# Four of the eleven gate-and-up pairs of each FFN by one level of Strassen's scheme

## The chip, the cores and the metric

The kernel runs on one core of a Trainium2 chip. Its time is the device time of one execution in microseconds (us); shorter is better. The engines that matter here are PE (TensorE, the matmuls), DVE (VectorE) and ACT (ScalarE), which work on tensors in on-chip memory, and the queues that issue transfers: SP (SyncE) for loads and POOL (GpSimd) for stores. Each engine goes through its own list of instructions in order, and waits where one needs what another engine or a transfer has not finished.

## The reference

Two decoder layers over 512 tokens of width 1024, all in float32. Layer 0 mixes tokens by causal pooling, layer 1 by differential attention; each layer ends in a feed-forward network (FFN) of 2816 hidden features. The change is in the FFN alone:

```python
def _swiglu(x, w_gate, w_up, w_down):
    return (jax.nn.silu(x @ w_gate) * (x @ w_up)) @ w_down

for i in range(DEPTH):
    mixed = pool(x) if i % 2 == 0 else diff_attention(x)
    x = _layernorm(ALPHA * x + mixed, ...)
    x = _layernorm(ALPHA * x + _swiglu(x, w_gate[i], w_up[i], w_down[i]), ...)
```

## The kernel before

**Precision.** Every float32 operand is split into a high part (a cast on ACT, L89) and a low part (a subtraction on DVE, L90); a product is three matmuls: high by high, high by low, low by high (`mm3`, L107 to L110).

**Layout.** Activations stand transposed: `xt` holds the layer's input as [feature of a block of 128, token half, high or low, block, 256 tokens]. The weights lie in `wall` as pieces of 128x1024. `fetch` loads a piece from `wall` on SP into one of RAWS = 4 `raw` tiles, `ready` splits it into one of WBUFS = 6 pairs of tiles `wh`, `wl`. A raw tile is free again once its piece is split, a pair of split tiles once the product that reads it is done.

**The FFN** (`ffn`, from L436) has two stages. In the first, the 2816 hidden features are 22 blocks `f` of 128, taken in pairs k and k + 11 (11 pairs). A block has one gate piece and one up piece; `product` multiplies each with all 512 tokens in 24 matmuls of 128x128 by 128x512 into one bank. `gated` applies silu on ACT (L459) and the multiply on DVE (L460) and leaves the block in `hid`. The first blocks ("early", 3 in layer 0, 2 in layer 1) are done in token halves of 256 columns, since the second half of the tokens comes late. The remaining blocks are the loop at L587; after a product it splits a further piece, five ahead.

In the second stage the down projection already runs by one level of Strassen's scheme: the seven products P1, Q5, P6, Q3, P7, P2, Q4, each over six groups of rows (`items`). What it needs is made during the first stage, in the shadow of PE's matmuls:

- `sum_weights(k)`: sums of quarters of the down weights for row block k. Four loads `b` on SP (L482), four DVE adds of 128x512 (L484), four stores to `tsum` in device memory on POOL's queue (L486). The four `b` tiles are single, so a load of one set waits for the store of the same tile in the set before. It runs for one k in every other feature, and besides at the first and the last of the loop (L597).
- `sum_hidden(k)`: sums of quarters of `hid` for pair k. A copy of one quarter to `a11` on ACT (L497), five DVE operations of 128x256 (L498 to L504), the cast `v` on ACT (L505), and, deferred to `settle` in the next feature, the low part on DVE (L508) and a store to `ssum` (L509).
- `affine`: scale and shift of the residual `res` by the layer norm's parameters, two DVE operations of 128x1024 (L189, L190) in each of the four features after the first of the loop.

In the down stage `prepare` fetches and splits the items five ahead, and `left` splits their left sides out of `hid` into `xt`, or loads them from `ssum`; for P1 `a11` is used as it stands.

The order on each engine is the order in which the code issues: nothing is reordered afterwards.

Of the kernel before, what the change touches and what calls it, by code (L numbers as in the profile page):

```python
# [45 lines left out]
DOWN = ("P1", "Q5", "P6", "Q3", "P7", "P2", "Q4")  # L46
PAIRS = [(0, 2), (2, 2), (4, 2), (6, 2), (8, 2), (10, 1)]
# [3 lines left out]
def trunk(ctx, tc, x, wall, pscale, lam_p, subln, table, lng, lnb, band, first, onehot, out):  # L51
# [381 lines left out]

    ROWS = [slice(k, k + n) for k, n in PAIRS]

    def ffn(layer, late):  # L436
        n = 2 * layer + 1
        final = n == 2 * DEPTH - 1
        c0 = base[0]
        with tc.tile_pool(name=f"ffn{layer}", bufs=1) as fp:  # L440


            hid = fp.tile([P, FB, S], F32, name=f"hid{layer}")
            a11 = fp.tile([P, 2, HALF, 256], F32R, name=f"a11_{layer}")

            def product(acc, c, lo, hi):
                h, l = weights(c)
                for k in range(KB):
                    mm3(
                        wide(acc, lo, hi),  # L450
                        (h[:, k * P : (k + 1) * P], l[:, k * P : (k + 1) * P]),
                        x_at(k, lo, hi),
                        k == 0,
                        k == KB - 1,
                    )

            def gated(f, pg, pu):
                sg = keep.tile([P, S], F32, tag="y", name=f"sg{layer}_{f}", bufs=2)
                nc.scalar.activation(sg, pg, AF.Silu)  # L459
                nc.vector.tensor_tensor(hid[:, f, :], sg, pu, op=ALU.mult)  # L460

            c1 = c0 + 2 * FB
# [11 lines left out]
            def sum_weights(k):  # L474

                i, j = k // 2, k % 2
                c = slice(j * 512, (j + 1) * 512)
                b11, b12, b21, b22 = t = [
                    fp.tile([P, 512], F32, tag=f"b{b}", name=f"b{b}_{layer}_{k}") for b in range(4)
                ]  # L480
                for b in range(4):
                    nc.sync.dma_start(out=t[b], in_=block(i, b)[:, c])  # L482
                for z, x, y in ((b11, b11, b12), (b12, b12, b22), (b22, b11, b22), (b21, b22, b21)):
                    nc.vector.tensor_tensor(z, x, y, op=ALU.add)  # L484
                for m, z in enumerate((b11, b22, b12, b21)):
                    nc.gpsimd.dma_start(out=tsum[m, i, :, c], in_=z)  # L486

            late_low = []
            summed_rows = [0]

            def sum_hidden(k):
                first, second = hid[:, k, :256], hid[:, k, 256:]
                a12, a22 = hid[:, k + HALF, :256], hid[:, k + HALF, 256:]
                u = fp.tile([P, 2, 256], F32, tag="u", name=f"u{layer}_{k}", bufs=1)
                v = fp.tile([P, 2, 2, 256], F32R, tag="v", name=f"v{layer}_{k}", bufs=1)
                tt = nc.vector.tensor_tensor
                nc.scalar.copy(a11[:, 0, k, :], first)  # L497
                tt(second, second, a22, op=ALU.subtract)  # L498
                tt(a11[:, 1, k, :], first, a11[:, 0, k, :].bitcast(F32), op=ALU.subtract)
                tt(first, second, first, op=ALU.subtract)  # L500
                nc.vector.scalar_tensor_tensor(
                    u[:, 0, :], first, -1.0, a22, op0=ALU.mult, op1=ALU.subtract
                )
                tt(u[:, 1, :], a12, first, op=ALU.add)  # L504
                nc.scalar.copy(v[:, :, 0, :], u)  # L505
# [11 lines left out]
            early = 3 if layer == 0 else 2  # L517
            accs = [(bank(f"g{layer}_{f}"), bank(f"u{layer}_{f}")) for f in range(early)]
            for lo in (0, 256):
                for f in range(early):  # L520
                    for i in range(2):
                        product(accs[f][i], c0 + 2 * f + i, lo, lo + 256)
                        if not lo and (f, i) in late:
                            late[f, i]()
                        if not lo:
                            ready(c0 + 2 * early)
                    if lo:
                        ready(c0 + 2 * f + 6)
                        gated(order[f], *accs[f])
            sum_hidden(0)  # L530
            if layer:
                load_gb(n - 1)
            items = [(p, i) for p in DOWN for i in range(len(PAIRS))]
            made, drops, prepared = {}, {}, [0, 0]
            fetched_items = [0]

# [19 lines left out]
            def left(j):  # L556
# [3 lines left out]
                if p == "P1":  # L560
                    made[j] += (a11[:, 0, r, :], a11[:, 1, r, :])
                    return
# [540 lines left out]
```

## Time and profile before

| what | before |
|---|---|
| time, median of 3 runs | 981.78 us (980.24 to 983.37) |
| the profiled execution's own time | 983.17 us |
| its span, first to last instruction | 981.1 us |
| mean granted clock of PE | 0.995 |
| PE busy | 963.2 us in 4974 matmuls |
| DVE busy | 643.4 us in 1007 instructions |
| ACT busy | 420.5 us in 708 instructions |
| loads of raw pieces (SP) | 128 of 512 KB, median 4.2 us from issue to landing |
| loads of `b` (SP) | 88 of 256 KB, median 5.6 us |

Layer 0's first stage runs from 40 to 284 us on PE. In a line of instructions "L90 DVE ... wl<-raw,wh" is line 90 of the kernel, the engine, and what is written and read; "x118 | 141.7, 1220 | 33.3" is 118 instances, 141.7 us busy in all, 1220 ns each, and 33.3 us in which the engine was idle just before them, with what ended that. In a timeline the first two columns are start and duration in us, and square brackets hold the idle time before.

### The profile page before, as it was taken

To read this page: it belongs to the slowest core of one execution; us is meant where nothing else is said; L and a number is where in the kernel's file an instruction comes from. 1 tells how busy PE (TensorE), PEld (TensorE's weight loads), DVE (VectorE), ACT (ScalarE), POOL (GpSimd) and SP (SyncE) were. 2 spreads that over 40 slices of the span, in tenths; PEclk is the share of its full clock that TensorE was granted. 3 is DMA by queue.
4 is the path that set the end of the run, shared out by engine and by line. 5 is a ranking of instruction groups with operands and counts; after the bars stand their busy time and mean duration, and the time that the engine had idled before them with its cause. 6 is when DMAs were issued, how large, how long until landed. Compare 5 with 4: busy or idle time off the path is not lost.

```text
span 981.1 us, 13416 instructions
## 1 busy us (share of the span) xinstructions
PE 963.2 (98%) x4974; PEld 820.6 (84%) x4974; DVE 643.4 (66%) x1007; ACT 420.5 (43%) x708; POOL 123.7 (13%) x195
## 2 busy tenths in 40 slices
PE   8999999999999999999999999999999999999995
PEld 8898888888888888988888888988888888888884
DVE  6845874455567577688777676756655555477687
ACT  5753222223326357656556554732223322244460
POOL 4201111111120211000000000011111111111102
PEclk9999999999999999999999999999999999999997
DMA  8247768655776984323222122276665566878942
GB/s 223 66 158 247 250 228 289 229 193 193 266 257 236 329 295 151 114 82 94 73 87 86 55 86 86 90 270 211 225 256 193 209 229 228 288 246 297 341 145 86
DMA packets 70079, 188.59 MB, mean 192 GB/s; under 512 B 15956, under 2 KB 16084, under 8 KB 70014
## 3 DMA queue, kind: packets, MB, share of 16 engines
q1 hardware_dynamic: 56588, 141.57, 42.1%
q0 software_dynamic: 13408, 46.15, 13.9%
q8 instruction: 39, 0.64, 0.3%
q14 instruction: 26, 0.21, 0.1%
q10 hardware_dynamic: 18, 0.02, 0.0%
HBM read 150.99 MB, written 36.72 MB: 191 GB/s over the span
## 4 chain that ended last, share of the span: by engine, by line
PE 94%; DVE 3%; ACT 1%; POOL 1%; issue 0%; POOLq 0%; DVEq 0%
PE P L629 13%; PE g L109 8%; PE u L108 8%; PE u L109 8%; PE g L108 8%; PE u L110 8%; PE g L110 8%; PE Q L629 6%; PE s L814 2%; PE v L108 2%; PE v L110 2%; PE v L109 2%; PE wo L108 2%; PE wo L109 2%; PE wo L110 2%; PE q L109 1%
## 5 line engine op out<-in xcount | busy, mean ns | idle before, releaser
L90 DVE TENSOR_TENSOR wl<-raw,wh 128x1024 fp32r<-128x1024 f32 x118 | 141.7, 1220 | 33.3 <-ACT wh L89 33.3
L89 ACT CAST wh<-raw 128x1024 fp32r<-128x1024 f32 x120 | 123.5, 1050 | 65.9 <-PE u L109 63.9
L109 PE MATMUL g<-xt,wh 128*128 128x512 f32 (+1 forms) x392 | 144.1, 368 | 0.5 <-DVE xt L90 0.5
L108 PE MATMUL g<-xt,wh 128*128 128x512 f32 (+1 forms) x392 | 144.3, 368 | 0.0
L108 PE MATMUL u<-xt,wh 128*128 128x512 f32 (+1 forms) x392 | 144.1, 368 | 0.0
L110 PE MATMUL u<-xt,wl 128*128 128x512 f32 (+1 forms) x392 | 144.0, 367 | 0.0
L109 PE MATMUL u<-xt,wh 128*128 128x512 f32 (+1 forms) x392 | 144.0, 367 | 0.0
L110 PE MATMUL g<-xt,wl 128*128 128x512 f32 (+1 forms) x392 | 144.0, 367 | 0.0
L460 DVE TENSOR_TENSOR hid<-sg,u 128x512 f32<-128x512 f32 x44 | 30.3, 688 | 154.9 <-PE u L110 154.5
L90 DVE TENSOR_TENSOR dl<-r,dh 128x1024 fp32r<-128x1024 f32 x84 | 94.3, 1132 | 38.8 <-ACT dh L89 38.7
L89 ACT CAST dh<-r 128x1024 fp32r<-128x1024 f32 x84 | 81.5, 979 | 69.6 <-PE P L629 31.7
L629 PE MATMUL P<-dh,xt 128*128 128x512 f32 x352 | 109.4, 390 | 0.0
L109 PEld LDWEIGHTS g<-xt,wh 128*128 128x128 f32 x392 | 73.9, 189 | 12.7 <-DVE xt L90 0.7
L110 PEld LDWEIGHTS u<-xt,wl 128*128 128x128 f32 x392 | 73.9, 189 | 12.3
L108 PEld LDWEIGHTS u<-xt,wh 128*128 128x128 f32 x392 | 73.9, 189 | 12.1
L110 PEld LDWEIGHTS g<-xt,wl 128*128 128x128 f32 x392 | 73.9, 188 | 12.2
L108 PEld LDWEIGHTS g<-xt,wh 128*128 128x128 f32 x392 | 73.9, 188 | 12.2
L109 PEld LDWEIGHTS u<-xt,wh 128*128 128x128 f32 x392 | 73.9, 188 | 12.0
L505 ACT CAST v<-u 128x512 fp32r<-128x512 f32 x22 | 13.7, 621 | 159.4 <-issue 142.5
L629 PEld LDWEIGHTS P<-dh,xt 128*128 128x128 f32 x352 | 66.1, 188 | 13.6
L484 DVE TENSOR_TENSOR b<-b,b 128x512 f32<-128x512 f32 x88 | 60.8, 691 | 18.4 <-DMA b<-in_wall 16.2
L459 ACT ACTIVATE sg<-g 128x512 f32<-128x512 f32 x44 | 26.3, 599 | 103.5 <-PE g L110 102.0
(189 smaller groups left out, 1792.5 us busy)
## 6 DMA issues: line engine op xcount, KB each, us to landing
raw<-in_wall SPq DMA_DIRECT2D x128, 512.0 KB, 4.2
b<-in_wall SPq DMA_DIRECT2D x88, 256.0 KB, 5.6
tsum<-b POOLq DMA_DIRECT2D x88, 256.0 KB, 4.7
r<-tsum SPq DMA_DIRECT2D x40, 512.0 KB, 4.7
r<-in_wall SPq DMA_DIRECT2D x30, 512.0 KB, 5.0
ssum<-v POOLq DMA_DIRECT2D x22, 512.0 KB, 4.0
xt<-ssum POOLq DMA_DIRECT2D x20, 512.0 KB, 6.0
res<-in_x SPq DMA_DIRECT2D x8, 256.0 KB, 6.4
```

The lines of the kernel that those rows point to most:

```text
L89: nc.scalar.copy(dst_h, src)
L90: (low or nc.vector).tensor_tensor(dst_l, src, dst_h.bitcast(F32), op=ALU.subtract)
L108: nc.tensor.matmul(acc, ah, bh, start=start, stop=False)
L109: nc.tensor.matmul(acc, ah, bl, start=False, stop=False)
L110: nc.tensor.matmul(acc, al, bh, start=False, stop=stop)
L459: nc.scalar.activation(sg, pg, AF.Silu)
L460: nc.vector.tensor_tensor(hid[:, f, :], sg, pu, op=ALU.mult)
L484: nc.vector.tensor_tensor(z, x, y, op=ALU.add)
L505: nc.scalar.copy(v[:, :, 0, :], u)
L629: nc.tensor.matmul(accs[s], x[:, k, r], y[:, c], start=first and k == 0 and e == 0, stop=last and k == m - 1 and e == 2, skip_group_check= ...
L814: nc.tensor.matmul(accs[c][:, :wide], a[r, qs], b[r, :wide], start=i == 0, stop=i == 2)
```

## The change

Pairs 4, 6, 8 and 9 of each layer compute gate and up of both their blocks by one level of Strassen's scheme; the other seven stay as they were, in between.

- The two by two scheme: token halves by input halves of `x`, and input halves by (gate, up) of the weights. A pair's four pieces are laid out by `layout` as gate and up of both blocks for one half of the input each. Seven products of 24 matmuls of 128x128 by 128x256 take the place of 96 of 128x512. The seven right sides are pieces or sums of pieces: `advance` adds raw pieces in place on DVE (L514, L516, L521, L526) and splits each result, so that a pair has seven splits instead of four, and two raw tiles are free only after P7, the other two after Q4.
- The left sides: quarters of `xt`, or sums of quarters in a new tensor `xs`, made once a layer by `sums_of_x`: four whole quarters (L568), four sums or differences (L578 to L590), four casts on ACT (L571) and four lows on DVE (L574), all of 1024 columns, with rows of `hid` as scratch. They run in the plain features behind the first of the loop, one step after each product.
- The banks: P1, P6, P7 and Q4 follow one another in bank A, Q5 and Q3 in C, P2 in B. ACT copies P1, Q5 and P6 out (L753, L755, L757), DVE adds or subtracts Q3, P7 and P2 (L759, L761, L763), then two silus (L764, L767) and two multiplies (L772, L774).
- `sum_weights` is issued in other places: one set in each early feature, one at the first of the loop, none while `affine` runs, and then in the plain features that are left, two in f=10. For k < 4 its four tiles are spare rows of `hid`, for k >= 4 one tile with the tag "gb" (which also holds the layer norm's parameters); `load_gb(n)` comes at the end of the stage.
- `sum_hidden` has four DVE operations and no copy; `a11` is gone, the lefts of P1 are split like the others and those of P6 take one more subtraction. The lefts of the down stage stand in `xs`.

```diff
+SPLIT = (4, 6, 8, 9)
+GATE = ("P1", "Q5", "P6", "Q3", "P7", "P2", "Q4")
...
+                    if p == "":
+                        drop = (c,)
+                    elif p == "Q5":
+                        tt(t, t, raws[c + 1], op=ALU.add)
+                    elif p == "P6":
+                        tt(t, t, raws[c + 2], op=ALU.add)
+                    elif p == "Q3":
+                        t = raws[c + 2]
+                    elif p == "P7":
+                        t = raws[c + 1]
+                        tt(t, t, raws[c + 2], op=ALU.add)
+                        drop = (c + 1, c + 2)
+                    elif p == "P2":
+                        t = raws[c + 3]
+                    elif p == "Q4":
+                        tt(t, t, raws[c + 3], op=ALU.add)
+                        drop = (c, c + 3)
...
             def sum_weights(k):
...
+                if k < 4:
+                    b11, b12, b21, b22 = t = [hid[:, row, :] for row in (9, 10, 20, 21)]
+                else:
+                    rest = keep.tile([P, 4, 512], F32, tag="gb", name=f"b{layer}_{k}")
+                    b11, b12, b21, b22 = t = [rest[:, q, :] for q in range(4)]
...
                     if lo:
+                        advance(2 * f + 6)
                         gated(order[f], *accs[f])
+                        sum_weights(next(weight_sums))
...
+            def plain(f):
...
                 for i in range(2):
+                    product(a[i], j + i, 0, S)
+                    ahead(j + i + 5)
+                    if f > early:
+                        next(steps, None)
                     if i == 0:
                         settle()
                 gated(order[f], *a)
                 if 0 < f - early <= SB:
                     affine(n - 1, f - early - 1)
+                elif f >= early:
+                    for _ in range(2 if f == 10 else 1):
+                        w = next(weight_sums, None)
+                        if w is not None:
+                            sum_weights(w)
+                if f % 2:
+                    sum_hidden(k)
+
+            def strassen(k):
...
+                for j, p in enumerate(GATE):
+                    acc = banks[names[p]]
...
+                    if p == "P1":
+                        g0 = tile_of(0)
+                        nc.scalar.copy(both(g0), acc)
+                    elif p == "Q5":
+                        nc.scalar.copy(second, acc)
+                    elif p == "P6":
+                        nc.scalar.copy(first, acc)
+                    elif p == "Q3":
+                        tt(first, acc, first, op=ALU.subtract)
...
+                    ahead(index[k] + j + 6)
...
+                sum_hidden(k)
```

How the order moves, at three places of layer 0. In the rows an operation's line comes first, then what it writes and reads; the numbers behind names count tiles.

DVE where the second half of the early features is done (`hid` by the multiply, `wl` or `gl` the low part of a weight piece). Before:

```order
L460 TENSOR_TENSOR hid_533<-sg_0_795,u_0_538 128x512
L90 TENSOR_TENSOR wl_849<-raw_514,wh_848 128x1024
L90 TENSOR_TENSOR wl_855<-raw_567,wh_854 128x1024
L460 TENSOR_TENSOR hid_533<-sg_11_858,u_1_540 128x512
L90 TENSOR_TENSOR wl_912<-raw_573,wh_911 128x1024
L90 TENSOR_TENSOR wl_918<-raw_846,wh_917 128x1024
L460 TENSOR_TENSOR hid_533<-sg_1_921,u_2_542 128x512
L498 TENSOR_TENSOR hid_533<-hid_533 128x256
L499 TENSOR_TENSOR a_0_534<-hid_533,a_0_534 128x256
L500 TENSOR_TENSOR hid_533<-hid_533 128x256
L501 SCALAR_TENSOR_TENSOR u_0_924<-hid_533 128x256
L504 TENSOR_TENSOR u_0_924<-hid_533 128x256
```

After:

```order
L555 TENSOR_TENSOR hid_533<-sg_0_795,u_0_538 128x512
L611 TENSOR_TENSOR hid_533<-hid_533 128x512 x4
L92 TENSOR_TENSOR gl_6_861<-raw_514,gh_6_860 128x1024
L92 TENSOR_TENSOR gl_7_867<-raw_567,gh_7_866 128x1024
L555 TENSOR_TENSOR hid_533<-sg_11_870,u_1_540 128x512
L611 TENSOR_TENSOR hid_533<-hid_533 128x512 x4
L92 TENSOR_TENSOR gl_8_936<-raw_573,gh_8_935 128x1024
L92 TENSOR_TENSOR gl_9_942<-raw_858,gh_9_941 128x1024
L555 TENSOR_TENSOR hid_533<-sg_1_945,u_2_542 128x512
L611 TENSOR_TENSOR hid_533<-hid_533 128x512 x4
```

A set of four weight sums (L611, in rows of `hid`) now stands behind each of the three multiplies, where there was none.

DVE in pair 5, the plain pair between the Strassen pairs 4 and 6 (`b_` the sums of weights, `raw` in front of the arrow a sum of raw pieces). Before:

```order
L484 TENSOR_TENSOR b_0_4_1541<-b_0_4_1541,b_0_4_1542 128x512
L484 TENSOR_TENSOR b_0_4_1542<-b_0_4_1542,b_0_4_1544 128x512
L484 TENSOR_TENSOR b_0_4_1544<-b_0_4_1541,b_0_4_1544 128x512
L484 TENSOR_TENSOR b_0_4_1543<-b_0_4_1544,b_0_4_1543 128x512
L90 TENSOR_TENSOR wl_1584<-raw_1456,wh_1583 128x1024
L460 TENSOR_TENSOR hid_533<-sg_5_1587,u_10_1508 128x512
L90 TENSOR_TENSOR wl_1619<-raw_1486,wh_1618 128x1024
L90 TENSOR_TENSOR wl_1649<-raw_1533,wh_1648 128x1024
L460 TENSOR_TENSOR hid_533<-sg_16_1652,u_11_1591 128x512
```

After:

```order
L555 TENSOR_TENSOR hid_533<-sg_5_1650,u_10_1594 128x512
L611 TENSOR_TENSOR b_4_1653<-b_4_1653 128x512 x4
L611 TENSOR_TENSOR b_5_1666<-b_5_1666 128x512 x4
L516 TENSOR_TENSOR raw_1483<-raw_1483,raw_1546 128x1024
L92 TENSOR_TENSOR gl_29_1707<-raw_1483,gh_29_1706 128x1024
L92 TENSOR_TENSOR gl_30_1735<-raw_1546,gh_30_1734 128x1024
L555 TENSOR_TENSOR hid_533<-sg_16_1738,u_11_1680 128x512
L611 TENSOR_TENSOR b_6_1741<-b_6_1741 128x512 x4
```

Three sets (b_4, b_5, b_6) stand where one stood.

SP's loads there, with their waits (DMASW are stores of POOL's queue, DMAHW earlier loads). Before:

```order
L482 DMA b_0_5_1698<-in_wall 128x512 [waits DMAHW2_49,DMASW5_49]
L482 DMA b_0_5_1699<-in_wall 128x512 [waits DMAHW3_49,DMASW7_49]
L482 DMA b_0_5_1700<-in_wall 128x512 [waits DMAHW4_49,DMASW0_49]
L482 DMA b_0_5_1701<-in_wall 128x512 [waits DMAHW5_49,DMASW6_49]
L79 DMA raw_1738<-in_wall 128x1024 [waits DMAHW6_49,DVE_49]
```

After:

```order
L609 DMA b_5_1666<-in_wall 128x512 [waits DMASW6_49,DMASW7_49,DMASW5_49,DMAHW4_49,DMASW0_49,DVE_49]
L609 DMA b_5_1666<-in_wall 128x512 [waits DMAHW5_49]
L609 DMA b_5_1666<-in_wall 128x512 [waits DMAHW6_49]
L609 DMA b_5_1666<-in_wall 128x512 [waits DMAHW7_49]
L609 DMA b_6_1741<-in_wall 128x512 [waits DMASW3_49,DMASW4_49,DMASW2_49,DMAHW0_49,DMASW1_49,DVE_49]
...
L81 DMA raw_1795<-in_wall 128x1024 [waits DMAHW4_49,DVE_49,Activation_49]
```

Before, a load of a set waits for one store; now the first load of a set waits for all four of the set before, and the raw pieces of the next plain pair stand behind the last set.

ACT from the end of pair 5 on (`v` the cast of `sum_hidden`, `A`, `C` the banks). Before:

```order
L459 ACTIVATE sg_16_1652<-g_11_1590 128x512
L497 CAST a_0_534<-hid_533 128x256
L505 CAST v_5_1656<-u_5_1655 128x2x256
L89 CAST wh_1692<-raw_1581 128x1024
L89 CAST wh_1740<-raw_1616 128x1024
L459 ACTIVATE sg_6_1744<-g_12_1664 128x512
```

After:

```order
L554 ACTIVATE sg_16_1738<-g_11_1679 128x512
L626 CAST v_5_1755<-u_5_1754 128x2x256
L753 COPY sg_6_0_1788<-A_6_1761 128x512
L91 CAST gh_31_1791<-raw_1514 128x1024
L91 CAST gh_32_1799<-raw_1579 128x1024
L755 COPY hid_533<-C_6_1762 128x2x256
L91 CAST gh_33_1831<-raw_1483 128x1024
L757 COPY hid_533<-A_6_1761 128x2x256
```

The copies out of the banks A and C stand behind the cast of `v_5`, which reads what the last add of `sum_hidden(5)` on DVE writes.

More of the change, by code (lines that the diff above doesn't have):

```diff
@@ L515, in settle @@
                     late_low.pop(0)()
[L517 to L535, printed above, removed]
-            def fetch_item(j):
-                p, i = items[j]
-                w = 512 * PAIRS[i][1]
-                t = keep.tile([P, 1024], F32, tag="raw", name=f"r{layer}_{j}", bufs=RAWS)[:, :w]
-                src = {"P1": 0, "P2": 2, "Q3": 3}
-                if p in src:
-                    nc.sync.dma_start(out=t, in_=block(i, src[p]))
-                else:
-                    m = {"Q5": 0, "P6": 1, "P7": 2, "Q4": 3}[p]
-                    nc.sync.dma_start(out=t, in_=tsum[m, i, :, :w])
-                drops[j] = t
             def split_item(j):
```

239 lines of the change are left out of this document (188 added, 51 removed).

## The prediction, made before the changed kernel was run

> **What bounds the kernel now.** I read the page's busy table, then its chain, then one feature of the chain piece by piece, then stretches of the gate-and-up stage.
>
> ```profile
> PE 963.2 (98%) x4974; PEld 820.6 (84%) x4974; DVE 643.4 (66%) x1007; ACT 420.5 (43%) x708; POOL 123.7 (13%) x195
> PE 94%; DVE 3%; ACT 1%; POOL 1%; issue 0%; POOLq 0%; DVEq 0%
> core 0: us, PE busy (x) PEld busy (x) DVE busy (x) ACT busy (x) POOL busy (x), PEclk, DMA share, GB/s
> 77.00:284.00 207.00, 207.00 (x916) 171.42 (x916) 119.81 (x168) 57.39 (x77) 29.25 (x52) 1.00 0.70 241
> 284.00:376.00 92.00, 92.00 (x405) 75.72 (x404) 67.48 (x83) 47.72 (x61) 10.88 (x16) 1.00 0.78 272
> ```
>
> The first two lines: PE (TensorE) is busy 98% of the span and makes up 94% of the chain that ended last. The windows are layer 0's whole-width gate-and-up features (77 to 284) and most of its down projection (284 to 376). PE has no idle time in either, so today fewer PE microseconds are a shorter kernel. But VectorE (DVE), the other engine with much to do, has 119.8 of 207 us busy in the first and 67.5 of 92 in the second. What is added to DVE in the features has 87 us of room on average; the question is where it lands.
>
> **The gain on PE.** The chain's piece of the first matmul of one feature and that of its second product, and matmuls 256 wide from the early features:
>
> ```profile
> 77.35 0.23 PE g L108
> ...
> 88.25 0.23 PE g L108
> 54.15 0.28 PE L108 MATMUL g<-xt,wh 128*128 128x256 f32 x1
> ...
> 65.67 0.28 PE L108 MATMUL g<-xt,wh 128*128 128x256 f32 x1
> ```
>
> Between the first two starts lie 48 matmuls of 512 columns: 10.90 / 48 = 0.227 us each. Between the other two lie 96 of 256 columns: 11.52 / 96 = 0.120 us, more than half of 0.227. A plain pair is 96 x 0.227 = 21.80 us, a Strassen pair 7 x 24 = 168 x 0.120 = 20.16. The gain is 1.64 us a pair, **13.1 us** for the eight pairs: 7.5% of their PE time, not the eighth that the count of products says. The Trainium skill, "TensorE: Matmul & The Clock Gate", section "Back-to-back issue gap", gives a warm gap of N/2.4 + 2.5 ns; by that estimate the pairs would save 8 x (20.72 - 18.34) = 19 us. The trace's pitches are 11 ns above the page's at both widths, so the trace's stand.
>
> **What DVE gets.** Prices of its operations and of the ACT (ScalarE) operations between them:
>
> ```profile
> L90 DVE TENSOR_TENSOR wl<-raw,wh 128x1024 fp32r<-128x1024 f32 x118 | 141.7, 1220 | 33.3 <-ACT wh L89 33.3
> L484 DVE TENSOR_TENSOR b<-b,b 128x512 f32<-128x512 f32 x88 | 60.8, 691 | 18.4 <-DMA b<-in_wall 16.2
> L460 DVE TENSOR_TENSOR hid<-sg,u 128x512 f32<-128x512 f32 x44 | 30.3, 688 | 154.9 <-PE u L110 154.5
> L190 DVE TENSOR_TENSOR res<-res,gb 128x1024 f32<-128x1024 f32 x12 | 14.7, 1226 | 0.4
> L504 DVE TENSOR_TENSOR u<-hid 128x256 f32<-128x256 f32 x22 | 9.2, 418 | 0.0
> L89 ACT CAST wh<-raw 128x1024 fp32r<-128x1024 f32 x120 | 123.5, 1050 | 65.9 <-PE u L109 63.9 <-issue 1.3 <-ACT line L422 0.7
> L505 ACT CAST v<-u 128x512 fp32r<-128x512 f32 x22 | 13.7, 621 | 159.4 <-issue 142.5 <-DVE u L504 16.9
> ```
>
> So any DVE operation of 1024 columns is 1.22 us, of 512 is 0.69, of 256 is 0.42; ACT takes 1.05 and 0.62 for 1024 and 512. Per layer the pairs bring 12 more split pieces and 16 sums of weights (28 x 1.22 = 34 us on DVE) and the sums of x another 12 x 1.22 = 14.6; `sum_hidden` loses one of its five adds (11 x 0.42 = 4.6). Some 44 us net against 87 of room: by averages it fits. By places it does not, for two reasons.
>
> First, `sum_weights`. Before, one set of four sums came in every other feature, about 21.8 us apart. Now layer 0 has sets b_0 to b_3 right after one another (three early features and f=3), then b_4 to b_6 in the two features of pair 5, b_7 and b_8 in those of pair 7, b_9 and b_10 in those of pair 10 (layer 1 has b_3 at f=7 instead). Each set reuses the tiles of the set before, so its loads wait for the stores of that set, and DVE, which runs in order, stands at its first sum meanwhile. The trace shows such a round trip twice, where two sets stand in consecutive features (3 and 4, 20 and 21 of layer 0):
>
> ```profile
> 83.45 2.87 DVE L484 TENSOR_TENSOR b<-b,b 128x512 f32<-128x512 f32 x4
> ...
> 95.69 0.69 DVE L484 TENSOR_TENSOR b<-b,b 128x512 f32<-128x512 f32 x1 [1.08 <-DMA b<-in_wall]
> 98.64 2.15 DVE L484 TENSOR_TENSOR b<-b,b 128x512 f32<-128x512 f32 x3 [2.26 <-DMA b<-in_wall]
> ...
> 268.61 2.86 DVE L484 TENSOR_TENSOR b<-b,b 128x512 f32<-128x512 f32 x4
> ...
> 279.31 0.69 DVE L484 TENSOR_TENSOR b<-b,b 128x512 f32<-128x512 f32 x1 [4.17 <-DMA b<-in_wall]
> 282.27 2.15 DVE L484 TENSOR_TENSOR b<-b,b 128x512 f32<-128x512 f32 x3 [2.26 <-DMA b<-in_wall]
> 85.89 1.60 POOL L486 DMA_DIRECT2D tsum<-b  x3 [0.22 <-issue]
> tsum<-b POOLq DMA_DIRECT2D x88, 256.0 KB, 4.7
> DMA to landing us min/median/max: 3.0/5.6/8.5
> DMA to landing us min/median/max: 2.3/4.7/10.9
> ```
>
> From the first sum of a set to that of the next are 95.69 - 83.45 = 12.2 and 10.7 us, and the second set lasts 5.1 us instead of 2.9, as its loads come in one by one. I take a round trip of 11.5 and a last set of 5.1 where each load waits for its own store (b_0 to b_3, in spare rows of `hid`). From b_4 on a set is one tile "gb", and the first load waits for all four stores: 2.87 of sums, 0.6 to the last store's issue (POOL's row: 85.89 to 87.49 for the last three, the sums end at 86.32, less 1.60 / 3 = 0.53 of the last issue), 4.7 to landing (the last line: stores; the one before: loads), 0.4 on SP and a load of 3.0 to 5.6: 11.6 to 14.2. I take 13, and 3.6 for the last set. The bounds are 9.2 (2.9 + 0.6 + 2.3 + 0.4 + 3.0, all minima, with sets of 2.9) and 12.2 and 17.1 (the second with a load of 8.5).
>
> Second, what waits for DVE. In a Strassen pair P1 and P6 share bank A, so P6 waits for ACT's copy of P1 (L753). In ACT's order that copy stands behind the cast `v` of the pair before (L626), and that behind the last add of `sum_hidden` on DVE (L625). So **PE, after P1 and Q5, waits until DVE has gone through its whole list up to that add**; the lookahead of five or six weight pieces doesn't help. Behind P6 in PE's order stands everything else.
>
> **Stalls, place by place**: DVE's list against PE's, from a common point, the end of a product that DVE's next operation waits for (0.8 us later its multiply is done).
>
> Pair 4, layer 0, from the end of feature 0's second half. DVE: 0.8 + 3 round trips 34.5 + last set 5.1, then 30 operations of 1024 columns (8 lows, 12 for the sums of x, 8 of affine, 2 sums of weights) 36.6, six of 512 4.1, three `sum_hidden` of four adds 5.3, and about seven waits for a cast of what DVE itself has just written, 1.4 each (1.05 for the cast and two handovers): 10. That is 56; with the two ACT operations (0.62 each) 97.6. PE: two half features 11.5, five features 54.5, P1 and Q5 5.8: 71.8. Stall **25.8**.
>
> Pair 4, layer 1 (two early features, so two round trips and set b_3 later, unhurried): 0.8 + 23 + 5.1 + 62 + 1.2 = 92.1 against 5.8 + 65.4 + 5.8 = 77.0. Stall **15.1**.
>
> Pair 6, either layer, from the end of f=10: 0.8 + 2 x 13 + 3.6 + sum_hidden 1.8 + 1.2 = 33.4 against one feature and P1, Q5: 16.7. Stall **16.7**.
>
> Pairs 8 and 9, from the end of f=14: 0.8 + 13 + 3.6 + 1.8, then pair 8's own list (13 of 1.22, six of 0.69, five waits, sum_hidden) 27.3, and 1.2: 47.7 against 10.9 + 20.2 + 5.8 = 36.9. Stall **10.8**, in whatever pieces.
>
> Besides, P7 needs A again, behind the copy of P6 (L757), which ACT reaches after the cast of a sum that DVE makes late: 1.1 in pairs 4 and 6, 2.2 a layer. The down stage's first items come after b_10: 0.8 + 13 + 3.6 and some 6 of adds, casts and lows against two products of f=21, 21.8: 2 a layer.
>
> On SP the raw pieces of the next plain pair stand behind the waiting loads of b (those of pair 7 behind b_6); PE needs them a whole Strassen pair, 20 us, later, so that costs nothing while R stays below that. The copies into `a11` (one of 256 columns on ACT and one on DVE, 11 a layer) go, the lefts of P1 (split anew) and P6 (one more subtraction) come, some 8 us of DVE a layer in the down stage: I cost it at nothing, for DVE has 92 - 67.5 = 24.5 us idle there; without that cover it costs 8 a layer.
>
> **The clock.** After an idle stretch PE's matmuls may run slower. The start of the trace and its end:
>
> ```profile
> 7.55 0.58 PE L311 MATMUL pool<-fh,xt 128*128 128x256 f32 x1 [1.01 <-ACT fh L89]
> ...
> 15.23 0.41 PE L315 MATMUL pool<-bh,xt 128*128 128x256 f32 x1
> ...
> 18.43 0.38 PE L316 MATMUL pool<-bh,xt 128*128 128x256 f32 x1
> 968.45 0.39 PE L629 MATMUL P<-dh,xt 128*128 128x512 f32 x1
> 966.00:971.00 5.00, 2.84 (x13) 2.03 (x11) 4.44 (x9) 0.00 (x0) 1.70 (x2) 1.00 0.28 105
> 971.00:976.00 5.00, 0.00 (x0) 0.00 (x0) 4.35 (x8) 0.00 (x0) 1.70 (x2) 0.50 0.28 105
> ```
>
> The last matmul ends at 968.84, and from 971 the granted clock is 0.50: some two idle microseconds are enough. At the start, 15 matmuls take 18.43 - 15.23 = 3.2 us, 0.213 each, some 11 us after the first one (18.43 - 7.55). Between nothing and 11 us at half rate (52 matmuls done instead of 92, 4.8 us lost) a long stall may cost; I take 2.5 for each of the four over 15 us: **+10**. The Trainium skill (that page, section "Part 1: The HAM clock gate (the "warmup" mystery)") says that an idle window of 3.4 us halves the clock and a busy one restores it: by that estimate four times 1.7, +7. The trace agrees on the half rate and shows a longer warming at the start.
>
> **The sum.** Layer 0: 25.8 + 16.7 + 10.8 + 2.2 + 2 = 57.5. Layer 1: 15.1 + 16.7 + 10.8 + 2.2 + 2 = 46.8. With the clock +114; less 13.1: +101. The profiled execution took 983.2 us (span 981.1 and 2 around it), so it becomes 1084; the median of the runs is 1.4 lower: **1083**.
>
> **Rivals.**
> *Short round trips*: all at 9.2 with sets of 2.9 and no cold clock. Pair 4: 16.7 and 8.3; pair 6: 8.4 each; pairs 8 and 9: 6.3 each; 54.4 + 8.4 - 13.1 = +50, 1032; half the way to the forecast, 1057. For it: the minima occurred. Against: both round trips in the trace were above 10.
> *Long round trips and a cold clock*: 12.2 and 17.1, and 4.8 after each stall: 124 + 8.4 + 19.2 - 13.1 = +139, 1120. For it: 70% of the DMA time is in use in these features already, and SP's loads of the next raws stand behind the waiting ones.
> *Faster: PE stays the bound.* 983.2 - 13.1 = 970, in the median 969. It is decided by the round trip R at the sets: pair 6 stalls 2R - 9.3, pair 4 3R - 8.7 and 2R - 7.9, pairs 8 and 9 R - 2.2; with the 8.4 of small ones all of it comes to less than 13.1 only below R = 3.6. For it: DVE has 87 us free in the stretch and five pieces of lookahead. Against: one shortest store and one shortest load alone are 5.3.
>
> **How the numbers follow.** Forecast 0.60 (1057 to 1100), short round trips 0.19 (1032 to 1057), long and cold 0.15 (1100 to 1120), PE-bound 0.05, a tie 0.01. The range from 1036 to 1120 leaves out the last two and the tails. Slower by over 0.3% (about what a measurement of this kernel can tell from no change) 0.94, within it 0.01, faster 0.05.
>
> **What would show it.** In the changed kernel PE is idle just ahead of the P6 products of pairs 4, 6 and 8 or 9, ended by ACT's copy out of bank A (L753), and that copy starts as soon as the cast of `v` (L626) ends. DVE's sums at L611 have idle time ended by the loads of b, some 8 us a set. The granted clock falls below 1.00 after the gaps; the pitch of the new matmuls elsewhere is 0.120. I'm wrong if L753's copies are done before Q5 ends, if sets follow one another within 6 us, or if the whole gap is at other products.

## The result, and the profile after

The changed kernel takes 1088.78 us in the median of six runs (1085.1 to 1091.1), before 982.54 (979.82 to 983.37): a ratio of 1.1087, 95% interval 1.106 to 1.1114. The profiled execution has a span of 1087.6 us. First the page's busy table and the chain's shares, then the layer-0 features in the window that was shown of before, all of the changed kernel:

```profile
PE 981.3 (90%) x5550; PEld 854.4 (79%) x5550; DVE 757.3 (70%) x1113; ACT 461.4 (42%) x754; POOL 125.4 (12%) x195
PE 15%; issue 5%; DVE 4%; DMA 3%; ACT 2%; POOL 1%; SPq 0%; DVEq 0%; POOLq 0%; ACTq 0%
core 0: us, PE busy (x) PEld busy (x) DVE busy (x) ACT busy (x) POOL busy (x), PEclk, DMA share, GB/s
77.00:284.00 207.00, 169.56 (x946) 149.11 (x945) 139.25 (x167) 59.22 (x74) 22.39 (x39) 0.92 0.48 167
```

PE is no longer the bound in this stretch: 169.6 of 207 us busy, where it had been 207, and its granted clock is 0.92 in the mean. VectorE isn't full either (139 of 207), and less DMA runs than before. No engine is short of capacity; they wait for one another. The shares of the chain add up to 30% only: followed back from the end it breaks off at 758 us, so it tells of the last 329 us alone, of which PE holds half.

The waits, in us in total, how many and the longest:

```profile
ACT v L626 <- DVE u L625: 99.7, 13, 20.1
PE A L744 <- ACT sg L753: 61.1, 8, 13.4
DVE hid L611 <- DMA hid<-in_wall: 32.0, 12, 5.5
DVE b L611 <- DMA b<-in_wall: 27.6, 13, 7.4
```

In the order of cause: VectorE stands at the sets of weight sums for their loads (the last two lines), ScalarE's cast `v` waits for VectorE (the first), and eight times (once a pair) PE waits for the copy of P1 out of bank A (the second). At pair 6 of layer 0 the links stand one under the other, in the timelines of VectorE, ScalarE and PE:

```profile
192.82 2.87 DVE L611 TENSOR_TENSOR b<-b 128x512 f32<-128x512 f32 x4
...
202.91 0.69 DVE L611 TENSOR_TENSOR b<-b 128x512 f32<-128x512 f32 x1 [7.23 <-DMA b<-in_wall]
...
213.62 0.69 DVE L611 TENSOR_TENSOR b<-b 128x512 f32<-128x512 f32 x1 [2.06 <-DMA b<-in_wall]
218.34 0.42 DVE L625 TENSOR_TENSOR u<-u,hid 128x256 f32<-128x256 f32 x1
218.84 0.62 ACT L626 CAST v<-u 128x512 fp32r<-128x512 f32 x1 [8.83 <-issue]
219.37 0.58 ACT L753 COPY sg<-A 128x512 f32<-128x512 f32 x1
220.00 0.80 PE L744 MATMUL A<-xs,gh 128*128 128x256 f32 x2 [11.29 <-ACT sg L753]
```

Three sets 10.1 and 10.7 us apart, the cast as the last add of `sum_hidden` (L625) ends, the copy right behind the cast, P6 right behind the copy, after 11.29 idle us.

By stages of PE (first gate matmul, first and last matmul of the down stage, and so on), in us, with four of the experiments below:

| kernel | to the first gate matmul | gate and up, layer 0 | down, layer 0 | mixer of layer 1 | gate and up, layer 1 | down, layer 1, to the end |
|---|---|---|---|---|---|---|
| before | 40.1 | 243.8 | 106.8 | 231.2 | 241.6 | 117.5 |
| changed | 37.5 | 294.5 | 115.8 | 231.0 | 283.1 | 125.7 |
| e1_no_pairs | 38.7 | 292.8 | 108.9 | 231.0 | 281.7 | 119.2 |
| e9_no_pairs_spread | 37.2 | 243.8 | 108.9 | 231.0 | 241.6 | 119.8 |
| e7_spread_ahead_later | 39.9 | 259.2 | 109.7 | 231.0 | 254.1 | 120.8 |
| e10_two_pairs | 37.3 | 240.3 | 109.3 | 231.1 | 238.1 | 117.6 |

The loss lies in the two gate-and-up stages (50.7 and 41.5) and, which the prediction had small, in the down stages (9.0 and 8.2).

### The profile page after: what moved, and what is told of

Same layout as the page of the kernel before. It is cut to its first block, busy times and chain, and to the rows that moved or that the text cites. A ratio compares the mean times of both kernels' runs of the same rounds, so it can differ in the third digit from the quotient of the medians.

```text
span 1087.6 us, 14660 instructions
## 1 busy us (share of the span) xinstructions
PE 981.3 (90%) x5550; PEld 854.4 (79%) x5550; DVE 757.3 (70%) x1113; ACT 461.4 (42%) x754; POOL 125.4 (12%) x195
## 5 line engine op out<-in xcount | busy, mean ns | idle before, releaser
L92 DVE TENSOR_TENSOR gl<-raw,gh 128x1024 fp32r<-128x1024 f32 x104 | 125.7, 1222 | 74.4 <-ACT gh L91 74.4
L91 ACT CAST gh<-raw 128x1024 fp32r<-128x1024 f32 x104 | 106.5, 1045 | 128.1 <-DVE raw L516 66.0
L808 PE MATMUL P<-dh,xs 128*128 128x512 f32 x440 | 139.5, 395 | 0.0
L744 PE MATMUL A<-xs,gh 128*128 128x256 f32 x256 | 59.2, 332 | 62.7 <-ACT sg L753 61.1
L808 PEld LDWEIGHTS P<-dh,xs 128*128 128x128 f32 x440 | 82.8, 188 | 19.5
L808 PE MATMUL P<-dl,xs 128*128 128x512 f32 x220 | 86.8, 395 | 0.0
L112 PE MATMUL g<-xt,gl 128*128 128x512 f32 (+1 forms) x200 | 77.8, 389 | 5.8 <-DVE gl L92 5.8
L110 PE MATMUL g<-xt,gh 128*128 128x512 f32 (+1 forms) x200 | 77.8, 389 | 3.7 <-ACT gh L91 3.7
L111 PE MATMUL g<-xt,gh 128*128 128x512 f32 (+1 forms) x200 | 77.7, 388 | 0.0
L112 PE MATMUL u<-xt,gl 128*128 128x512 f32 (+1 forms) x200 | 76.3, 381 | 0.0
L111 PE MATMUL u<-xt,gh 128*128 128x512 f32 (+1 forms) x200 | 76.1, 381 | 0.0
L110 PE MATMUL u<-xt,gh 128*128 128x512 f32 (+1 forms) x200 | 76.1, 381 | 0.0
L611 DVE TENSOR_TENSOR b<-b 128x512 f32<-128x512 f32 x56 | 38.7, 692 | 28.9 <-DMA b<-in_wall 27.6
L92 DVE TENSOR_TENSOR wl<-raw,wh 128x1024 fp32r<-128x1024 f32 x38 | 46.0, 1220 | 9.4 <-ACT wh L91 9.3
```

Of the source, the lines that this page charges most:

```text
L91: nc.scalar.copy(dst_h, src)
L92: (low or nc.vector).tensor_tensor(dst_l, src, dst_h.bitcast(F32), op=ALU.subtract)
L110: nc.tensor.matmul(acc, ah, bh, start=start, stop=False)
L111: nc.tensor.matmul(acc, ah, bl, start=False, stop=False)
L112: nc.tensor.matmul(acc, al, bh, start=False, stop=stop)
L611: tt(z, x, y, op=ALU.add)
```

## The experiments

The theory was that the bunched sets of weight sums hold VectorE, and VectorE's list holds PE through bank A. The rivals: the Strassen pairs' own work; that the sets wait not for stores but in SP's queue; and, for the sizes, the clock. Times are medians of runs beside runs of the kernel before on the same chip (981.0 to 981.6).

**No pairs at all.**

```diff
-SPLIT = (4, 6, 8, 9)
+SPLIT = ()
```

> No pair by Strassen's scheme (SPLIT is empty); the sets of weight sums, the sums of x and everything else stay where the change put them. Theory 'sets' (VectorE stands at the bunched sets of weight sums, and PE is held by VectorE's list): the waits of 4 to 7 us at the sets stay, PE now waits at the low parts of weights instead of at bank A, some 25 to 30 us a layer: 1035 to 1055 us, though no pair is split. Rival 'pairs' (the pairs' own sums, splits and the chain through bank A are the loss): 980 to 995 us.

1071.23 us (ratio 1.0916, 1.0889 to 1.0944). Without a single Strassen pair 90 of the 106 us remain, and the gate-and-up stages take what they took in the changed kernel (292.8 and 281.7). So the pairs' own work is not the larger part of the loss; the theory had even expected too little of the sets. VectorE's second set behind feature 10 and PE, of this kernel:

```profile
212.57 0.69 DVE L611 TENSOR_TENSOR b<-b 128x512 f32<-128x512 f32 x1 [7.58 <-DMA b<-in_wall]
218.17 0.79 PE L112 MATMUL g<-xt,gl 128*128 128x512 f32 x1 [11.84 <-DVE gl L92]
```

The gap is as long as at pair 6 before (11.84 to 11.29), only that PE now waits for a low part of a plain pair's weights. Bank A is the place where PE meets VectorE's backlog, not its cause.

**Two sets of tiles in turn.**

```diff
-                if k < 4:
-                    b11, b12, b21, b22 = t = [hid[:, row, :] for row in (9, 10, 20, 21)]
+                if k < 4 or k in (5, 7):
+                    spare_rows = (7, 8, 18, 19) if k in (1, 3) else (9, 10, 20, 21)
+                    b11, b12, b21, b22 = t = [hid[:, row, :] for row in spare_rows]
```

> Successive sets of weight sums alternate between two sets of tiles (spare rows of hid for the odd early sets and for b_5, b_7), so that a load does not wait for the stores of the set just before. Theory 'sets', as predicted, with round trips set by those stores: the gaps ahead of pair 4 (23 and 15 us with what comes before them) fall below half and those of pair 6 (11.3, 13.4) to 2 or 3: 1040 to 1055 us. Rival 'queue' (in the early features the loads of b stand on SP behind loads of raw pieces that wait for VectorE's own low parts): pair 4 unchanged, pair 6 falls by 8 to 10 a layer: 1062 to 1070. Rival 'pairs': 1085 to 1090.

1063.1 us (1.0834, 1.0816 to 1.0851). PE in this kernel ahead of P6 of pairs 4 and 6:

```profile
162.37 0.80 PE L745 MATMUL A<-xs,gh 128*128 128x256 f32 x2 [11.63 <-ACT sg L754]
208.74 0.50 PE L745 MATMUL A<-xs,gh 128*128 128x256 f32 x2 [2.64 <-ACT sg L754]
```

Pair 6 falls from 11.29 to 2.64, so its sets did wait for the stores. Pair 4 doesn't move (11.62 before): there the prediction had the wrong waiter, and time and place are those of rival 'queue'. SP and VectorE of the changed kernel at the fourth set (VectorE's previous one had started at 85.73):

```profile
84.40 11.09 SPq L81 DMA_DIRECT2D raw<-in_wall  x2
95.58 1.82 SPq L609 DMA_DIRECT2D hid<-in_wall  x4
101.76 0.69 DVE L611 TENSOR_TENSOR hid<-hid 128x512 f32<-128x512 f32 x1 [4.29 <-DMA hid<-in_wall]
```

SP stands 11 us at two loads of raw pieces, whose slots VectorE's own low parts free, and only then issues the loads of the set, for which VectorE waits.

**The loads a set ahead.** The loads move into a function of their own, which is also called for the next set before the adds of this one, and so stands on SP ahead of the raw pieces between the two.

```diff
+                load_weights(k)
+                if k + 1 < HALF and where_b[k + 1] != where_b[k]:
+                    load_weights(k + 1)
```

> The sets of weight sums stay where the change put them, with alternating tiles as in the run with two sets of tiles, and the loads of the next set are issued on SP ahead of the raw pieces that stood in front of them, one set early. Theory 'queue' (in the early features the sets wait because their loads stand on SP behind raw pieces that wait for VectorE): the waits of 4 to 5 us at the early sets go and the gaps ahead of pair 4 shrink from 11.6 and 10.9 (P6) by 5 to 10 us: 1040 to 1052 us against 1063 with the two tiles alone. Rival 'stores' (alternating tiles were all there was to gain): 1059 to 1066. Rival: the early loads push the raw pieces back and PE waits for these: above 1066.

1045.53 us (1.0661, 1.063 to 1.0692), 17.6 below the run before it. VectorE at the first two sets, and PE at P6 of pair 4:

```profile
64.06 2.87 DVE L625 TENSOR_TENSOR hid<-hid 128x512 f32<-128x512 f32 x4
69.83 2.87 DVE L625 TENSOR_TENSOR hid<-hid 128x512 f32<-128x512 f32 x4
149.00 0.79 PE L758 MATMUL A<-xs,gh 128*128 128x256 f32 x2 [10.30 <-ACT sg L767]
```

The second set follows after 5.8 us instead of 10.6, with no wait, so the queue was the waiter there. The time is where theory 'queue' put it, but not at the place it named: the gaps ahead of pair 4 (2.78, 2.23 and 5.04) are gone, that at P6 is still 10.30. By VectorE's timeline, which is idle for 4 of the 28 us before, it belongs to the rest of the list there: sums of x, affine, and the pair's own sums; no run takes these away alone. (In this run and in the runs with four and three pairs below, some sets stand in rows of `hid` that the sums of x write over before the adds, so part of the down weights' sums are others; amount and order of work are the same.)

**The cast later.**

```diff
-                nc.scalar.copy(v[:, :, 0, :], u)
                 def rest():
+                    nc.scalar.copy(v[:, :, 0, :], u)
```

> The cast v of sum_hidden stands on ScalarE behind the copy of P1 out of bank A instead of ahead of it (it moves to settle). Theory 'chain' (P6 waits for that copy, and the copy for VectorE's list through the cast): the gaps at P6 of pairs 4, 6 and 9 lose what VectorE does between P6's own low part and the last add of sum_hidden, some 2 to 5 us each, and what is left moves to P7: 1065 to 1080 us. Rival (the low parts of P6's weights are as late as the cast): 1085 to 1091.

1075.0 us (1.0956, 1.0926 to 1.0986), 14 less than the changed kernel. PE's waits in this kernel:

```profile
PE C L744 <- ACT hid L755: 31.7, 8, 9.9
PE A L744 <- ACT sg L753: 14.8, 6, 3.8
```

The waits at P1's copy fall from 61.1 to 14.8 us, and 31.7 come up at Q3, which waits for the copy of Q5 out of bank C: on ScalarE that copy stands behind casts of which one needs a sum of raw pieces (L521) from VectorE. I had expected the rest at P7. The chain through the cast is real; what stands behind it is the same backlog.

**The adds on GpSimd.**

```diff
-                    tt(z, x, y, op=ALU.add)
+                    nc.gpsimd.tensor_tensor(z, x, y, op=ALU.add)
```

> The four adds of a set of weight sums run on GpSimd in place of VectorE (a low part of 128x512 took 1.29 us there); nothing else moves. Theory 'sets': VectorE neither waits for b nor adds (30 us a layer less work): pair 6's gap falls from 11.3 and 13.4 to 5 or less, pair 4's by half, 1030 to 1050 us. Rival 'pairs': above 1070 us. Rival 'contention' (GpSimd's adds slow VectorE's operations): the mean of VectorE's low part of 1024 columns rises above 1.3 us from 1.22 and half of the gain is lost.

1084.23 us (1.1035, 1.0985 to 1.1084): little gained. 'Sets' missed. The time is in the range of 'pairs', but the run without pairs speaks against that cause; 'contention' is what the trace shows. Groups of this kernel:

```profile
L92 DVE TENSOR_TENSOR gl<-raw,gh 128x1024 fp32r<-128x1024 f32 x104 | 133.5, 1297 | 103.7 <-ACT gh L91 103.7
L91 ACT CAST gh<-raw 128x1024 fp32r<-128x1024 f32 x104 | 106.7, 1046 | 125.9 <-DVE raw L516 37.5 <-DVE raw L526 29.6 <-DMA raw<-in_wall 24.6
L611 POOL TENSOR_TENSOR b<-b 128x512 f32<-128x512 f32 x56 | 97.9, 1748 | 63.6 <-DMA b<-in_wall 60.5
```

VectorE's low part takes 1.297 us on average instead of 1.222: 1.52 for the 26 that run while GpSimd adds, 1.22 for the 78 others. Over the whole kernel 60.9 us of adds left VectorE (88 of 0.69), and its other operations became 46.9 us longer, so that three quarters of the relief was lost. Besides, the casts now wait 24.6 us for raw pieces instead of 8.5: on SP these stand behind loads of b, which wait for the stores of the set before, and GpSimd takes 7.3 us for the adds of a set instead of 2.9. What each of the two costs in time this run doesn't say.

**PE kept warm.** In the gaps stand matmuls on data that nobody reads.

```diff
+                    for i in range({(0, 4, "P1"): 24, (0, 4, "P6"): 80, (0, 6, "P6"): 80, (0, 9, "P6"): 36,
+                                    (1, 4, "P6"): 76, (1, 6, "P6"): 92, (1, 9, "P6"): 36}.get((layer, k, p), 0)):
+                        nc.tensor.matmul(banks["B"][:, :256], xt[:, 0, 0, 0, :P], xt[:, 0, 0, i % 4, :],
+                                         start=True, stop=True, skip_group_check=True)
```

> In the gaps of PE ahead of the products at bank A of pairs 4, 6 and 9 stand 24 to 92 matmuls of 128x256 on data that nobody reads, fewer than the gap holds; nothing else moves. Theory 'clock' (the matmuls at half clock behind the gaps cost time, 54 us of them in the changed kernel, some 25 us lost, of which what is lost behind a gap and not ahead of the next counts, 12 to 16): 1070 to 1079 us, and the stretches of clock 0.50 go at these gaps. Rival (PE waits for VectorE again anyway, so a slow PE costs nothing): 1085 to 1092.

1083.87 us (1.1037, 1.1009 to 1.1065), 4.9 less than the changed kernel. Two stretches of the changed kernel, then the same two of this one (columns as in the windows above, the granted clock behind POOL):

```profile
156.00:169.60 13.60, 5.43 (x25) 5.43 (x26) 12.07 (x14) 5.25 (x8) 0.71 (x1) 0.50 0.22 77
842.00:855.60 13.60, 5.39 (x25) 5.39 (x26) 9.52 (x13) 3.81 (x6) 2.86 (x5) 0.50 0.58 208
```

```profile
156.00:169.60 13.60, 11.56 (x97) 11.35 (x96) 12.02 (x14) 5.25 (x8) 0.71 (x1) 1.00 0.26 77
842.00:855.60 13.60, 12.24 (x100) 11.83 (x100) 11.13 (x12) 8.05 (x10) 0.72 (x1) 1.00 0.77 264
```

In these two the clock stays at 1.00, and the gain is below the 12 to 16 us expected; the intervals of the two ratios just overlap. Behind the kernel's start, 196 matmuls of the changed kernel start at half clock, 83 of this one, which at their prices is some 10 us less. Whether a slow PE costs its whole lost time where VectorE is behind stays open: between P6 of pair 4 and P6 of pair 6 layer 0 won 0.5 us (55.83 to 55.34) and layer 1 won 3.1 (57.79 to 54.73), with 25 and 24 half-clock matmuls fewer, worth 2.3 each.

**Everything mended, the same four pairs.** Loads ahead, the cast later, and one set in 20 us or so: in plain features as before the change, in each Strassen pair one behind Q5.

```diff
                     if i == 0:
                         settle()
+                        if f % 2 == 0 or f in (early, FB - 1):
+                            sum_weights(next(weight_sums))
...
                     ahead(index[k] + j + 6)
+                    if p == "Q5":
+                        sum_weights(next(weight_sums))
```

> The same four pairs, but one set of weight sums every 20 us or so (as before the change in the plain features, one in each Strassen pair behind Q5), loads one set ahead, the cast v behind the copy of P1. Theory 'sets and pairs' (the sets are the larger part; what is left is that a Strassen pair has 25 to 27 us of VectorE's work and waits in 20 us of PE's, and that the sums of x and affine crowd ahead of pair 4): 1010 to 1030 us. Rival 'sets alone': 970 to 985. Rival 'pairs alone': above 1050.

1016.11 us (1.0344, 1.0317 to 1.037). Two thirds of the loss are gone. What is left is at pair 4 of both layers and in pairs 8 and 9, which follow one another (of layer 0, P6 and Q3 of pair 4 and Q4 of pair 8):

```profile
142.44 0.80 PE L754 MATMUL A<-xs,gh 128*128 128x256 f32 x2 [5.15 <-ACT sg L763]
151.66 0.79 PE L754 MATMUL C<-xs,gh 128*128 128x256 f32 x2 [3.73 <-ACT hid L765]
...
249.40 0.51 PE L754 MATMUL A<-xt,gh 128*128 128x256 f32 x2 [2.63 <-DVE hid L771]
```

**The same without pairs.** This run keeps the sums of x and sets `SPLIT = ()`.

> No pair by Strassen's scheme, as in the first run, but with the weight sums one set every 20 us or so, loads a set ahead where the next set has tiles of its own, and the cast v later; the sums of x are still made. Theory 'sets and pairs': with neither, the gaps of the first stages go altogether and what is left above before is the down stages (7 to 9 us): 984 to 992 us; so of the first run's 90 us over before about 80 were the sets. Rival (the sums of x or affine crowd VectorE by themselves): above 1000 us.

984.31 us (1.0035, 1.0024 to 1.0045), and both gate-and-up stages take what they took before to a tenth of a us. With the first run and the one above it makes a square: with the sets as the change has them, 1071 without and 1089 with pairs; with the sets spread, 984 and 1016. The sets are 87 us without pairs and 73 with them; the four pairs cost 18 and 32 where they should have saved 13. "The sets" stands for three things here that the two runs change together: where the sets stand, loads ahead, and the cast later.

**Three pairs, each between plain ones**, with affine in features 4, 6, 8 and 12 and the lefts of the down stage from the ninth item on in `xt`:

```diff
-SPLIT = (4, 6, 8, 9)
+SPLIT = (5, 7, 9)
...
+                if j >= 8:
+                    o = 2 * (j % 4)
+                    t = xt[:, (1 + j // 4) % 2 if final else 1, :, o : o + m, :]
```

> As the run before it in the list, with pairs 5, 7 and 9 by Strassen's scheme, each with a plain pair on both sides, affine in features 4, 6, 8 and 12, and the lefts of the down stage from the ninth item on in xt again. Theory 'sets and pairs': each Strassen pair finds VectorE caught up; the gaps fall below 2 us each, and of 6 x 1.64 = 9.8 us saved on PE about half is kept: 974 to 980 us. Rival (VectorE's work doesn't fit even so): 985 to 1000. Rival (the gaps vanish and something else takes the gain back): 980 to 984.

987.32 us (1.0051, 1.0033 to 1.0069). The gaps of four pairs are gone but for one in pair 7 of each layer, where the set behind Q5 waits for its loads and Q4 for VectorE:

```profile
213.08 0.80 PE L757 MATMUL A<-xt,gh 128*128 128x256 f32 x2 [2.96 <-DVE hid L774]
```

It is 3.08 in layer 1; 27 matmuls at half clock follow the one in layer 0 (2.5 us), and the down stages are 3.5 and 2.6 us longer than before: together 14.6, more than the 9.8 us saved. The theory missed, and the time is in the range of the rival by which VectorE's work doesn't fit. The trace says so of one place only, the set behind Q5 of pair 7; whether the rest fits, the next run bears on.

**Two pairs, 6 and 8**, the sets in them behind P2, in tiles that nothing else uses by then.

```diff
+SPLIT = (6, 8)
+            where_b = 'AAAAABAGAGG'
...
+                    if p == {6: 'P2', 8: 'P2'}.get(k):
+                        sum_weights(next(weight_sums))
```

> Pairs 6 and 8 by Strassen's scheme, each with a plain pair on both sides; one set of weight sums in 20 us or so, none of them in tiles that the sums of x still use, in the two pairs behind P2; loads a set ahead where the tiles differ; cast v later; lefts of the down stage from the ninth item on in xt. Theory 'sets and pairs': the gaps of the first stages stay under 1 us each; 4 x 1.64 = 6.6 us are saved there and some 5 to 6 us lost in the down stages, as in the run with three pairs: 979 to 984 us, level with before. Rival (a Strassen pair always leaves PE waiting): 988 or more. Rival (the down stage's loss comes with the number of pairs): below 978.

**975.28 us** (0.9935, 0.9923 to 0.9948): faster than the kernel before, and better than expected: it is in the range of the rival on the down stage. The gate-and-up stage of its layer 0, in the columns of the windows:

```profile
37.30:277.60 240.30, 239.81 (x1362) 211.51 (x1361) 170.89 (x218) 90.00 (x125) 32.78 (x57) 1.00 0.63 217
```

PE is busy but for 0.5 us. The stages of the two layers take 240.3 and 238.1 us, 3.5 less than before in each, 1.75 a pair. VectorE is busy 171 of 240 us, a larger share than in the changed kernel's window (139 of 207), and PE doesn't wait for it. The down stage of layer 0 is 2.5 longer than before, that of layer 1 is not, where three pairs had 3.5 and 2.6. Since the sets and affine stand elsewhere too, the two runs don't show that the number of pairs makes this difference, nor which of the changes makes this kernel the faster one.

## Why the prediction held, step by step

The time came out 6 us above the forecast, well inside the range, and by the mechanism that was named: sets that follow one another hold VectorE, and P6 waits for P1's copy, that for the cast, that for VectorE. Not every term was right, and that the sum came so close is luck in part. PE's gaps against the terms, in us (the page's idle times ahead of the first matmul of a product, those over 0.5 added up by place):

| term | predicted, layer 0 / 1 | measured, layer 0 / 1 |
|---|---|---|
| pair 4 and what lies ahead of it | 25.8 / 15.1 | 22.9 / 15.5 |
| pair 6 | 16.7 / 16.7 | 11.3 / 13.4 |
| pairs 8 and 9 | 10.8 / 10.8 | 8.5 / 8.9 |
| P7 in pairs 4 and 6 | 2.2 / 2.2 | none over 0.5 |
| start of the down stage | 2 / 2 | 3.5 / 4.3 |
| sum | 57.5 / 46.8 | 46.2 / 42.1 |

- **The gain on PE** was right: 1.64 us a pair forecast, 1.75 measured where nothing else disturbs it (two pairs).
- **The round trip** was taken as 13 us from b_4 on and was 10.1 and 10.7 (10.2 and 12.8 in layer 1): the term of pair 6 is mis-sized by that, twice. The stores of the sets landed after 2.7 us in the median, not the 4.7 that I took from before; the lower bound of the range had the shorter time in it.
- **What the early sets wait for** was wrong, though the size came out: the prediction let each load wait for its own store; the runs with two tiles and with loads ahead show that loads stood on SP behind raw pieces. The fourth set came 16 us after the third (101.76 - 85.73), not 11.5. That the term came out is luck.
- **"By places it does not [fit], for two reasons"**: the first alone, the sets, is enough. The second, P6 behind the copy behind the cast, was priced as if it made the stall. The run without pairs shows the same stall in plain features; the chain through the cast is worth 14 us by the run that takes it away.
- **Pairs 8 and 9** came near, but not by the sets: VectorE waited 0.4 us at b_8 in layer 0 and 0.8 in layer 1. The 5.72 us ahead of P6 of pair 9 are pair 8's own list, which took 28.3 us (27.3 in the prediction; its own prices, with 1.4 for each wait, make 28.8) against 20 of PE's; with two sets of tiles and with loads ahead that gap stayed at 5.7. So what one pair asks of VectorE does hold up the next one where two pairs touch.
- **VectorE's added work** was taken as 44 us a layer. A gate-and-up stage has 51.7 and 52.2 us more: the three operations that take Q3, P7 and P2 out of the banks, 12 x 0.69 = 8.3 a layer, were left out of that sum, though not out of the lists place by place.
- **The waits at the sets** were to be some 8 us each: they are 2.8 to 9.8 at the sets that follow another up to the loop's first feature and at b_5 and b_6, and below 1.7 at b_8 and b_10.
- **The lefts of the down stage** were costed at nothing, and VectorE did have the time: without pairs, with the same lefts, the down stages were 2.1 and 1.7 us longer than before, which is the slower matmuls told of below (2.2 a layer). The 9.0 and 8.2 of the changed kernel are these, the half clock (2.8 and 1.4), and the start (3.5 and 4.3), forecast as 2 and for VectorE's list behind b_10. What PE waited for there is a load: SP's loads of `r` stand behind that of `gb`, whose tile b_10 holds until its stores land.

```profile
337.07 1.60 POOL L613 DMA_DIRECT2D tsum<-b  x3 [1.77 <-DVE b L611]
341.09 0.33 SPq L141 DMA_DIRECT2D gb<-in_lng  x1
349.46 1.04 ACT L91 CAST dh<-r 128x1024 fp32r<-128x1024 f32 x1 [6.43 <-DMA r<-tsum]
```

- **The clock** was mis-sized: 10 us forecast. Leaving out the stretch at the kernel's start, 159 matmuls 256 wide ran at 0.213 instead of 0.120 and 37 of 512 at 0.427 instead of 0.227: 159 x 0.093 + 37 x 0.2 = 22 us. The short gaps of 3 to 6 us, which I had not counted, slowed PE as well.
- The errors cancel: 16 us less of gaps, 12 more of clock and 4 of slower matmuls. Gaps 88, clock 22, pitch 4, less 13.1 make 101 of the 106.5 us of span; the rest I can't place.

The kernel with two pairs has 32.8 and 31.7 us more of VectorE's work in a gate-and-up stage than the kernel before. It fits there, where no two sets and no two pairs touch.

## What to carry to other kernels

Room on an engine's average says nothing when its list holds waits: count, in its order, from one wait of the next engine to the next. A load that waits (for its tile, or behind one that does) stopped every load behind it on SP's queue here, so loads for work that has time belong ahead of loads that wait, into tiles that are free by then. And a scheme that trades matmuls for vector work pays only where the vector engine catches up between two uses: two spread pairs won 0.65%, four of which two touch lost 3.4% with the sets spread, and 11% with the sets bunched as well.

## What the runs showed of the hardware

The pitch of a matmul, from start to start, changed with the tile that its stationary operand comes from. In the run with two pairs the first items of the down stage have their lefts in `xs`, the next ones in `xt`, with the same shapes (PE's timeline, the first matmul of each part and one later):

```profile
277.63 0.40 PE L823 MATMUL P<-dh,xs 128*128 128x512 f32 x1
...
298.55 0.39 PE L823 MATMUL Q<-dh,xt 128*128 128x512 f32 x1
...
316.01 1.03 PE L823 MATMUL P<-dh,xt 128*128 128x512 f32 x2
```

Ninety matmuls take 20.92 us, 0.2324 each; the next 77 take 17.46, 0.2268. Before, only the first 66 matmuls of a down stage (lefts in `a11`) had the slower pitch; in the changed kernel, leaving out waits and half clock, all 462 have it: 396 x 0.0056 = 2.2 us a layer. The reason wasn't looked for.

Half clock came in stretches of 3.4, 6.8, 10.2 and 13.7 us, multiples of 3.4, in the changed kernel's trace; an idle gap of 2.48 us was followed by one (from 763.5 on), one of 2.23 was not. The Trainium skill, "TensorE: Matmul & The Clock Gate", section "Part 1: The HAM clock gate (the "warmup" mystery)", has a free-running window of 3413 ns, which these lengths agree with. The idle 3.4 us that the prediction took from that section were not needed: the gap of 2.48 us was enough. The 1.7 us for a stall that the prediction worked out from it are what one such window costs, and the long stalls here cost more, since 1.2 to 1.6 windows pass before the clock is back (P6 starts at 164.17 and 220.00, half clock ends at 169.6 and 224.2).

GpSimd's adds and VectorE's operations slowed one another down in the run with the adds on GpSimd. The 10 adds that no VectorE operation overlaps took 1.28 us in the mean, the 35 that VectorE overlaps from end to end 1.85. VectorE's low parts of 128x512 into `xs` took 1.41 us beside an add (6 of them) and 0.69 else (44), but its multiplies L555 of the same width, which read one operand from a bank, 0.69 either way (11 and 17).
